# RWKV-7 scan on one core: fewer, fuller TensorE visits per slot, and new positions for transpositions and for the inversion

## The chip, the core and the metric

The kernel runs on one core of one Trainium2 chip. The metric is the device time of one execution in microseconds (us). Before the change the median of three runs is 2085.17 us (2083.7 to 2086.77).

The engines are called as the profile calls them: PE is TensorE (matmuls; PEld its weight loads), DVE is VectorE, ACT is ScalarE, POOL is GpSimd, SP is SyncE, which issues the DMAs.

## The reference, cut to what matters

Two layers on x of shape (1, 512, 2048). Layer 0 is attention and a pooling mixer and isn't touched. Layer 1 is RWKV-7 time mixing with 32 heads of 64 channels; its heart is a recurrence over the 512 tokens:

```python
def step(state, inp):                      # per head: state is 64 x 64
    r_t, w_t, k_t, v_t, kk_t, a_t = inp
    sa = jnp.einsum('bhvk,bhk->bhv', state, -kk_t)
    state = (state * w_t[:, :, None, :]
             + sa[..., None] * (kk_t * a_t)[:, :, None, :]
             + v_t[..., None] * k_t[:, :, None, :])
    return state, jnp.einsum('bhvk,bhk->bhv', state, r_t)
```

After it come a group norm per head, a bonus term, a gate and an output projection.

## The kernel before

**Stages.** Layer 0 and the projections for r, k and g fill the first 1400 us or so. Then comes `scan`, which takes the 32 heads as 16 pairs (two heads of 64 channels fill 128 partitions) and the 512 tokens as 8 chunks of 64. The projection for v is done inside the scan, as filler for PE. The output projection follows.

**What a pair needs.** Per pair q there are these pieces of work, each a Python generator whose steps are called *visits* here:

- `gprod(q)` (line 894): loads AR and BK, and makes the products BK x AR per chunk (line 908, tile `g`, two PSUM banks of four chunks, one bank per head), masked by DVE into `Z` (line 914); then transposes BK on PE (line 920, tile `bt`) and ACT copies it to `BT` (line 921).
- `lanes(q)` (line 945): the first level of inverting the 64 x 64 triangular matrices, in blocks of 16. POOL gathers the blocks from Z into `nd` with four instructions (line 950: two need the Z of one head, two that of the other), DVE transposes `nd` into `lt` (line 955), adds it up to `la`, then fifteen rounds of a product `pr` (line 962) and a sum `uc` (line 963), each of which needs the one before. ACT writes `e` (line 969), DVE transposes it to `tb` (line 971), ACT makes `DT` in two instructions (line 973), DVE transposes DT into `U` (line 977).
- `levels(q)` (line 981): the other two levels, four groups of small matmuls: q1, c1, q2, c2 (lines 1000 and 1010), with ACT and DVE in between. q1 needs DT.
- `vproj(q)` (line 875): the v projection, eight visits of six matmuls (lines 145 to 147, tile `vps`). `vprep(q)` transposes v. `post(q)` does group norm, transposition (`ot`, line 1104) and gate.
- `chain(q)` (line 1029): the recurrence over the eight chunks, which can't be moved. Each chunk takes three positions: **first** `xo` from state M and RS (lines 1044, 1047), copied to `xs` by DVE and then ACT (1051, 1052); **second** `sa` (1055), copied to `RS` by DVE (1056); **third** `s` (1062), from which DVE makes the new M in four instructions (1071), and the outputs `xo` (1076).

**Order of the work.** `slot` (line 1165) goes through 12 positions. At each it emits the next step of the running chains (the second half of pair p and the first half of pair p+1), with high priority, and then all planned visits whose number falls in that position. So positions 0, 3, 6, 9 hold xo and xs, positions 1, 4, 7, 10 hold sa and RS, positions 2, 5, 8, 11 hold s and M. `plan` (line 1161) spreads n visits evenly between two numbers, counted from the slot in which the pair's g begin; numbers from 12 on fall in the slot behind, so that in one slot the g of pair q+1 stand beside the levels of pair q. PE keeps the order in which the code emits; DVE, ACT and POOL are ordered by a list scheduler when the kernel is built, and each engine works through its own list strictly in that order. There are 13 slots in which two chains run and g, lanes, levels and v stand between them (1455 to 1836 us of the trace), one before them with a single chain, and two behind.

Positions of PE's visits in such a slot, by the old numbers: g at 0, 1, 3 and 4 (two chunks of each bank per visit); bt at 6 and 7; q1, c1, q2, c2 at 5, 7, 9, 10; v at 0, 2, 3, 5, 6, 8, 9, 11; ot at 5; the transposition of v at 11.

Of the kernel before, what the change touches and what calls it, by code (L numbers as in the profile page):

```python
# [8 lines left out]
F32 = mybir.dt.float32  # L9
F32R = mybir.dt.float32r  # L10
# [7 lines left out]
P = 128  # L18
S = 512
# [8 lines left out]

PO, LA, VP, LV, GP, VJ = (13.5, 20), (8, 15), (21.5, 25), (16, 24.5), (0.5, 9), (5.5, 17)
Q14, A13, B13, A14, B14, A15, B15, Q15 = (0, 3), (0.5, 5.5), (6, 12), (0, 10), (3, 12), (0, 9), (0.5, 11.5), (0, 11.5)


class Kernel:
# [809 lines left out]
    def scan(self, ctx, xv, first, mp, ld, ar_d, bk_d, bc_d, g_d, m_d):  # L845
# [8 lines left out]
        st = ctx.enter_context(tc.tile_pool(name="set", bufs=3))  # L854
# [39 lines left out]
        def gprod(p):  # L894

            s = sets[p]
            AR = s["AR"] = ld.tile([P, 8, 2, 64], F32, tag="AR", name="AR", bufs=4)
            nc.sync.dma_start(AR.rearrange("p a b c -> p (a b c)"), ar_d[p])
            BK = ld.tile([P, 8, P], F32, tag="BK", name="BK")
            nc.sync.dma_start(BK.rearrange("p a b -> p (a b)"), bk_d[p])  # L900
            yield

            Z = s["Z"] = [st.tile([P, 8, P], F32, tag=f"Z{h}", name=f"Z{h}", bufs=4) for h in range(2)]
            for b in range(2):
                g = [aux("g").rearrange("p (c n) -> p c n", c=4) for _ in range(2)]
                for c in range(4):
                    for h in range(2):
                        mm(g[h][:, c, :], BK[half[h], 4 * b + c, :],  # L908
                           AR[half[h], 4 * b + c].rearrange("p a b -> p (a b)"), start=True, stop=True)
                    if c == 1:  # L910
                        yield
                for h in range(2):
                    mk = self.mk[:, 64 * (p % 2):64 * (p % 2) + P]
                    nc.vector.tensor_mul(Z[h][:, 4 * b:4 * b + 4, :], g[h], mk.unsqueeze(1).to_broadcast([P, 4, P]))
                yield
            BT = s["BT"] = st.tile([P, 8, P], F32, tag="BT", name="BT")
            for b in range(2):
                g = aux("bt")
                for c in range(4):
                    nc.tensor.transpose(g[:, c * P:(c + 1) * P], BK[:, 4 * b + c, :], self.ident)  # L920
                nc.scalar.copy(BT[:, 4 * b:4 * b + 4, :], g.rearrange("p (c n) -> p c n", c=4))
                yield
# [58 lines left out]
        def levels(p):  # L981

            U, DT = (sets[p][n] for n in ("U", "DT"))
            ev = lambda t: t.rearrange("p c (b z t) -> p c b z t", b=2, z=2)[:, :, :, 0, :]
            od = lambda t: t.rearrange("p c (b z t) -> p c b z t", b=2, z=2)[:, :, :, 1, :]
            b2 = lambda g: g.rearrange("p c (b t) -> p c b t", b=2)
            N1 = tp.tile([P, 8, 64], F32, tag="N1", name="N1")

            Z, own, odd = sets[p]["Z"], p % 2, 64 * (p % 2)
            nc.scalar.copy(N1[half[1 - own]], Z[1 - own][half[own], :, odd:odd + 64])  # L990
            N = [N1, N1]
            N[own] = Z[own][:, :, odd:odd + 64]
            yield

            def prod(name, L, R, K=0, n=64, m=0):
                g = pi.tile([P, 8, 32], F32, tag="i", name=name)
                for c in range(8):
                    for h in range(2):
                        kr, mr = slice(64 * h + K, 64 * h + K + n), slice(64 * h + m, 64 * h + m + n)
                        mm(g[mr, c, :], L[h][kr, c, 64 - n:64] if L is N else L[kr, c], R[kr, c], start=True, stop=True)  # L1000
                return g

            g = b2(prod("q1", N, ev(DT)))
            for b in range(2):
                nc.scalar.activation(q1z[:, :, 32 * b:32 * b + 16], g[:, :, b, :], AF.Copy, scale=self.om[:, b:b + 1])
            yield
            g = pi.tile([P, 8, 32], F32, tag="i", name="c1")
            for c in range(8):
                for h in range(2):
                    mm(g[64 * h:64 * h + 48, c, :], q1z[half[h], c, :48], od(U)[half[h], c], start=True, stop=True)  # L1010
            for h in range(2):
                r = slice(64 * h, 64 * h + 48)
                nc.vector.tensor_add(od(U)[r], od(U)[r], b2(g)[r])
            UT = tp.tile([P, 8, 32], F32, tag="UT", name="UT")
            nc.vector.transpose(UT, U[:, :, :32])
            yield
            g = prod("q2", N, UT, 0, 32, 32)
            q2 = tp.tile([P, 8, 32], F32, tag="q2", name="q2")
            for h in range(2):
                r = slice(64 * h + 32, 64 * h + 64)  # L1020
                nc.scalar.copy(q2[r], g[r])
            yield
            g = prod("c2", q2, U[:, :, 32:], 32, 32, 0)
            for h in range(2):
                r = slice(64 * h, 64 * h + 32)
                nc.vector.tensor_add(U[r, :, 32:], U[r, :, 32:], g[r])
            yield

        def chain(p):
# [3 lines left out]
            s = sets[p]  # L1033
            AR, RS, U, BT, Z = (s[n] for n in ("AR", "RS", "U", "BT", "Z"))
            O = s["O"] = tp.tile([P, 4, 2, 64], F32, tag="O", name="O", bufs=3)
# [3 lines left out]
            for c in range(8):  # L1039
# [19 lines left out]
                if c < 7:  # L1059
                    s1 = po.tile([P, 64], F32, tag="o", name="s1")  # L1060
                    for h in range(2):
                        mm(s1[half[h], :], BT[:, c, 64 * h:64 * h + 64], RS[:, c, h, :], start=True, stop=True)  # L1062
                    Mn = Ms[own * 2 + c % 2]
# [57 lines left out]
        wo = {}  # L1121

        def units(*ks):
            for k in ks:
                tag = "AR,Z0,Z1,AR,Z0,Z1,BT,RS,AR,Z0,Z1,BT,RS,BK,AR,Z0".split(",")[k]
                pool = ld if tag in ("AR", "BK") else st
                w = pool.tile([P, 2, S], F32R, tag=tag, name="wo", bufs=1 if k == 13 else 4 if tag[-1] in "R01" and tag != "RS" else 3)
                raw = self.wp.tile([P, S], F32, tag="wraw", name="wraw", bufs=3)
                nc.sync.dma_start(raw, Wo[k * P:(k + 1) * P, 0:512])
                self.split(w[:, 0, :], w[:, 1, :], raw)  # L1130
                if k not in mixed:
                    kk = [q for q in (k, k + 1) if q < 13]
                    ml = ld.tile([P, 2, S], F32, tag="BK", name="ml")
                    for n, q in enumerate(kk):
                        nc.sync.dma_start(ml[:, n, :], m_d[q])
                        mixed[q] = mp.tile([P, 2, S], F32R, tag="mx", name="mixed")
                        self.split(mixed[q][:, 0, :], mixed[q][:, 1, :], ml[:, n, :])
                wo[k] = w
                yield
# [19 lines left out]
        todo = []  # L1159

        def plan(base, g, n, a, b):

            todo.extend((base + a + (b - a) * q / n, len(todo), g) for q in range(n))
# [12 lines left out]
        def hurry(g):  # L1176
            while True:
                with tc.high_priority(offset=400):
                    if next(g, g) is g:
                        return  # L1180
                yield

        def plan_pair(base, q, skip=0):

            gp = gprod(q)
            next(gp)
            plan(base, gp, 6, *GP)
            plan(base, hurry(lanes(q)) if q == 15 else lanes(q), 18, *LA)
            plan(base, hurry(levels(q)) if q == 15 else levels(q), 5, *LV)
            plan(base, vproj(q), 8, *VJ)  # L1190
            plan(base, vprep(q), 2, *VP)


        v, gp = vproj(0), gprod(0)
        next(gp)
        for q in range(3):
# [3 lines left out]
        for q in range(16):  # L1200
            next(la)
            if q % 2:
                next(v, None)
        g1, v = gprod(1), vproj(1)
        next(g1)
        run(la)
        for q in range(6):
            next(g1)
            if q % 2:
                next(v)  # L1210
        run(vprep(0))
# [7 lines left out]
                next(v)  # L1219
        run(l0)  # L1220
        plan(-12, la, 12, 12, LA[1])
        plan(-12, levels(1), 5, *LV)
        plan(-12, vprep(1), 2, *VP)
        A = None
        for p in range(-1, 16):
# [20 lines left out]
        g = post(15)  # L1246
# [89 lines left out]
```

## Time and profile before

| what | value |
|---|---|
| median of three runs | 2085.17 us |
| the profiled execution, its own time | 2082.76 us |
| span in its trace | 2081.1 us |
| PE, PEld, DVE, ACT, POOL busy | 97%, 79%, 62%, 46%, 14% of the span |
| the 13 full slots of the scan | 1455.0 to 1836 us, 29.3 us each |
| granted TensorE clock, mean | 0.992 |

A row of the timeline has the start, the duration, the engine, the line, the operation, output <- inputs and shapes; merged rows carry xcount, and brackets tell how long the engine had idled before it and what released it. A row of the waits tells who waited for whom: the sum in us, how often, the longest. A row of the groups ends with busy time, mean ns of one, and the idle time ahead of it with its releasers. Matmuls are pipelined, so the time from the start of one visit to the start of the next is what a visit costs on PE.

### The profile page before, as it was taken

How to read it: one execution, taken by the hardware profiler on the slowest of the kernel's cores; microseconds unless marked ns; L12 is line 12 of the kernel's file. 1: busy time of each engine (PE TensorE's matmuls, PEld its weight loads, DVE VectorE, ACT ScalarE, POOL GpSimd, SP SyncE). 2: the span in 40 equal slices, each digit the busy share in tenths (PEclk: the TensorE clock that was granted, in tenths of full speed). 3: DMA queues.
4: the chain of work that ended last, by engine and by line, in shares of the span. 5: the costliest groups of instructions: out<-in, count | busy, mean ns of one | idle time of the engine just before them, and what ended most of it. 6: DMA issues, size and time to landing. Idle time of an engine off the chain costs nothing. (4 is left out here: it accounts for less than half of the span.)

```text
span 2081.1 us, 33937 instructions
## 1 busy us (share of the span) xinstructions
PE 2015.5 (97%) x13091; PEld 1635.0 (79%) x13091; DVE 1281.4 (62%) x2572; ACT 960.2 (46%) x1687; POOL 282.9 (14%) x550
## 2 busy tenths in 40 slices
PE   8999999999999998999999999999999999989996
PEld 7888888888888897777878888876777777767786
DVE  4344345444433358666866676668788888876336
ACT  3345445323322138654645564454565555564221
POOL 0000000000000000234000000013444444410003
PEclk9999999999999999999999999999999999999998
DMA  5222222233333353465365556542223332332733
GB/s 195 92 81 81 81 81 66 86 97 99 99 111 112 117 167 125 143 179 175 118 212 194 177 174 218 197 164 67 81 84 108 108 108 84 101 113 97 245 104 111
DMA packets 214033, 262.99 MB, mean 126 GB/s; under 512 B 15768, under 2 KB 161776, under 8 KB 213104
## 3 DMA queue, kind: packets, MB, share of 16 engines
q1 hardware_dynamic: 213872, 260.83, 38.9%
q8 instruction: 103, 1.69, 0.3%
q14 instruction: 58, 0.48, 0.1%
HBM read 214.32 MB, written 46.47 MB: 125 GB/s over the span
## 5 line engine op out<-in xcount | busy, mean ns | idle before, releaser
L141 DVE TENSOR_TENSOR wlo<-wraw,whi 128x1024 fp32r<-128x1024 f32 (+1 forms) x268 | 314.7, 1177 | 464.3 <-ACT whi L137 455.9
L137 ACT CAST whi<-wraw 128x1024 fp32r<-128x1024 f32 (+1 forms) x324 | 302.9, 938 | 538.3 <-PE ga L146 299.6
L145 PE MATMUL ga<-mx,whi 128*128 128x512 f32 x768 | 299.8, 391 | 3.9 <-ACT mx L137 3.9
L146 PE MATMUL ga<-mx,whi 128*128 128x512 f32 x768 | 300.2, 391 | 2.1 <-DVE mx L141 2.1
L145 PE MATMUL ga<-x,whi 128*128 128x512 f32 x768 | 300.5, 391 | 1.0 <-ACT whi L137 1.0
L147 PE MATMUL ga<-mx,wlo 128*128 128x512 f32 x768 | 300.0, 391 | 0.0
L147 PE MATMUL ga<-x,wlo 128*128 128x512 f32 x768 | 299.4, 390 | 0.5 <-DVE wlo L141 0.5
L146 PE MATMUL ga<-x,whi 128*128 128x512 f32 x768 | 299.2, 390 | 0.0
L508 PE MATMUL gb<-wlo,mixed 128*128 128x512 f32 (+1 forms) x576 | 196.9, 343 | 1.8 <-DVE wlo L141 1.8
L506 PE MATMUL gb<-whi,mixed 128*128 128x512 f32 (+1 forms) x576 | 197.4, 343 | 1.1 <-DVE s L457 1.1
L507 PE MATMUL gb<-whi,mixed 128*128 128x512 f32 (+1 forms) x576 | 196.9, 342 | 0.0
L145 PEld LDWEIGHTS ga<-mx,whi 128*128 128x128 f32 x768 | 144.7, 188 | 36.6 <-ACT mx L137 4.1
L146 PEld LDWEIGHTS ga<-mx,whi 128*128 128x128 f32 x768 | 144.7, 188 | 33.7 <-DVE mx L141 2.8
L147 PEld LDWEIGHTS ga<-x,wlo 128*128 128x128 f32 x768 | 144.2, 188 | 31.2 <-DVE wlo L141 1.0
L147 PEld LDWEIGHTS ga<-mx,wlo 128*128 128x128 f32 x768 | 144.6, 188 | 30.5
L145 PEld LDWEIGHTS ga<-x,whi 128*128 128x128 f32 x768 | 144.2, 188 | 30.6 <-ACT whi L137 1.3
L146 PEld LDWEIGHTS ga<-x,whi 128*128 128x128 f32 x768 | 144.3, 188 | 29.1
L141 POOL TENSOR_TENSOR wlo<-wraw,whi 128x128 fp32r<-128x128 f32 x224 | 100.3, 478 | 222.1 <-ACT whi L137 196.7
L508 PEld LDWEIGHTS gb<-wlo,mixed 128*128 128x128 f32 x576 | 109.1, 190 | 15.8 <-DVE wlo L141 3.4
L506 PEld LDWEIGHTS gb<-whi,mixed 128*128 128x128 f32 x576 | 109.1, 190 | 15.3 <-DVE s L457 2.8
L507 PEld LDWEIGHTS gb<-whi,mixed 128*128 128x128 f32 x576 | 109.2, 190 | 12.3
L145 PE MATMUL vps<-mx,whi 128*128 128x512 f32 x256 | 113.4, 443 | 0.8 <-ACT vT L891 0.8
(333 smaller groups left out, 3345.4 us busy)
## 6 DMA issues: line engine op xcount, KB each, us to landing
wraw<-in_ev_w_in SPq DMA_DIRECT2D x96, 512.0 KB, 3.6
wraw<-in_ev_w_out SPq DMA_DIRECT2D x32, 512.0 KB, 3.6
wraw<-in_od_w_k SPq DMA_DIRECT2D x32, 512.0 KB, 4.7
wraw<-in_od_w_r SPq DMA_DIRECT2D x32, 512.0 KB, 3.4
wraw<-in_od_w_g SPq DMA_DIRECT2D x32, 512.0 KB, 3.8
wraw<-in_od_w_v SPq DMA_DIRECT2D x64, 256.0 KB, 2.7
ar_d<-pAR SPq DMA_DIRECT2D x16, 512.0 KB, 2.6
bk_d<-pBK SPq DMA_DIRECT2D x16, 512.0 KB, 3.3
```

Of the source, the lines that this page charges most:

```text
L137: self.nc.scalar.copy(hi, src)
L141: (eng or self.nc.vector).tensor_sub(lo[:, sl], src[:, sl], hi[:, sl].bitcast(F32))
L145: mm(ps, ah, bh, start=start, stop=False)
L146: mm(ps, ah, bl, start=False, stop=False)
L147: mm(ps, al, bh, start=False, stop=stop)
L506: mm(ps, ah, bh, start=start, stop=False)
L507: mm(ps, al, bh, start=False, stop=False)
L508: mm(ps, ah, bl, start=False, stop=stop)
```

## The change

The new kernel has its lines one further down from the table on (line 909 for 908, 1055 for 1056). It does four things.

- g: the yield after the second chunk goes, so one visit makes four chunks of both banks. gprod has four visits and no longer six; they get written-out positions 1.5, 3.3 (g) and 5.45, 6.9 (bt), the latter two just ahead of v's visits at 5.5 and 6.94.
- levels: written-out positions 15.5, 16.5, 19.5, 21.1, 22.5, so q1, c1, q2, c2 stand at 4, 7, 9 and 10 of a slot.
- lanes: 18 visits spread from 6.5 to 14.5, before from 8 to 15.
- BT gets four buffers, before three (4 KB more per partition); the output projection's tiles that share its tag follow.

```diff
-PO, LA, VP, LV, GP, VJ = (13.5, 20), (8, 15), (21.5, 25), (16, 24.5), (0.5, 9), (5.5, 17)
+PO, LA, VP, VJ = (13.5, 20), (6.5, 14.5), (21.5, 25), (5.5, 17)
+LV, GP = (15.5, 16.5, 19.5, 21.1, 22.5), (1.5, 3.3, 5.45, 6.9)
...
                         mm(g[h][:, c, :], BK[half[h], 4 * b + c, :],
                            AR[half[h], 4 * b + c].rearrange("p a b -> p (a b)"), start=True, stop=True)
-                    if c == 1:
-                        yield
...
-            BT = s["BT"] = st.tile([P, 8, P], F32, tag="BT", name="BT")
+            BT = s["BT"] = st.tile([P, 8, P], F32, tag="BT", name="BT", bufs=4)
...
+        def at_(base, g, *where):
+
+            todo.extend((base + x, len(todo), g) for x in where)
...
-            plan(base, gp, 6, *GP)
+            at_(base, gp, *GP)
             plan(base, hurry(lanes(q)) if q == 15 else lanes(q), 18, *LA)
-            plan(base, hurry(levels(q)) if q == 15 else levels(q), 5, *LV)
+            at_(base, hurry(levels(q)) if q == 15 else levels(q), *LV)
```

**PE, position 1 of the slot in which pair 7 ends and pair 8 begins** (`sa` products, then `g`, then `s`). Before:

```order
L1055 MATMUL sa<-xs_10978,U 64x128
L1055 MATMUL sa<-xs_10977,U 64x128
L908 MATMUL g<-AR,BK 128x128 x4
L1062 MATMUL s_14927<-RS,BT 64x64 x2
L1062 MATMUL s_14934<-RS,BT 64x64 x2
```

Now:

```order
L1054 MATMUL sa<-xs_10978,U 64x128
L1054 MATMUL sa<-xs_10977,U 64x128
L909 MATMUL g<-AR,BK 128x128 x8
L1061 MATMUL s_14936<-RS,BT 64x64 x2
L1061 MATMUL s_14943<-RS,BT 64x64 x2
```

The visit between sa and s has all eight products of the two banks; the visit of four at position 0 is gone.

**DVE, positions 2 to 5 of a slot.** Before, from tb to the xs of position 6 (the xs of position 3 stand ahead of these rows):

```order
L971 STREAM_TRANSPOSE tb<-e 128x512
L1056 COPY RS<-sa 64x128 x2
L914 TENSOR_TENSOR Z_14435<-g,mk 128x512
L1071 SCALAR_TENSOR_TENSOR M_10980<-s_14564,pcs,m_14567 64x64 x2
L1071 SCALAR_TENSOR_TENSOR M_10982<-s_14571,pcs,m_14574 64x64 x2
L977 STREAM_TRANSPOSE U<-DT 128x512
L914 TENSOR_TENSOR Z_14436<-g,mk 128x512
L955 STREAM_TRANSPOSE lt<-nd_10975 128x512
L1051 COPY xs_10977<-xo 64x64
L1051 COPY xs_10978<-xo 64x64
```

Now, from tb to the M of position 5 (the xs here are those of position 3):

```order
L970 STREAM_TRANSPOSE tb<-e 128x512
L1050 COPY xs_10977<-xo 64x64
L1050 COPY xs_10978<-xo 64x64
L221 SCALAR_TENSOR_TENSOR rsygn<-rstgn,rssgn 128x8
L1099 TENSOR_TENSOR O<-O,rsygn 128x512
L976 STREAM_TRANSPOSE U<-DT 128x512
L913 TENSOR_TENSOR Z_14459<-g,mk 128x512
L913 TENSOR_TENSOR Z_14460<-g,mk 128x512
L1055 COPY RS<-sa 64x128 x2
L954 STREAM_TRANSPOSE lt<-nd_10975 128x512
L1070 SCALAR_TENSOR_TENSOR M_10980<-s_14583,pcs,m_14586 64x64 x2
L1070 SCALAR_TENSOR_TENSOR M_10982<-s_14590,pcs,m_14593 64x64 x2
```

U and both Z have moved ahead of the chain's RS, the two Z stand next to each other, and lt has moved ahead of the chain's M; before, lt had only the xs of the next position behind it. On ACT the second DT now stands behind the two copies xs of position 3; before, no xs stood between the two DT.

More of the change, by code (lines that the diff above doesn't have):

```diff
@@ L1126, in units @@
                 pool = ld if tag in ("AR", "BK") else st
-                w = pool.tile([P, 2, S], F32R, tag=tag, name="wo", bufs=1 if k == 13 else 4 if tag[-1] in "R01" and tag != "RS" else 3)
+                w = pool.tile([P, 2, S], F32R, tag=tag, name="wo", bufs=1 if k == 13 else 3 if tag == "RS" else 4)
                 raw = self.wp.tile([P, S], F32, tag="wraw", name="wraw", bufs=3)
@@ L1181, in hurry, with plan_pair @@
                 yield
-        def plan_pair(base, q, skip=0):
+        def at_(base, g, *where):
+            todo.extend((base + x, len(todo), g) for x in where)
+        def plan_pair(base, q):
             gp = gprod(q)
             next(gp)
-            plan(base, gp, 6, *GP)
+            at_(base, gp, *GP)
             plan(base, hurry(lanes(q)) if q == 15 else lanes(q), 18, *LA)
-            plan(base, hurry(levels(q)) if q == 15 else levels(q), 5, *LV)
+            at_(base, hurry(levels(q)) if q == 15 else levels(q), *LV)
             plan(base, vproj(q), 8, *VJ)
@@ L1207, in scan @@
         for q in range(6):
-            next(g1)
+            next(g1, None)
             if q % 2:
@@ L1221, in scan @@
         plan(-12, la, 12, 12, LA[1])
-        plan(-12, levels(1), 5, *LV)
+        at_(-12, levels(1), *LV)
         plan(-12, vprep(1), 2, *VP)
```

## The prediction

> **What bounds the kernel now.** I read the page first, then cut out the scan, the only stage that the change touches, and asked who waits for whom there.
>
> ```profile
> PE 2015.5 (97%) x13091; PEld 1635.0 (79%) x13091; DVE 1281.4 (62%) x2572; ACT 960.2 (46%) x1687; POOL 282.9 (14%) x550
> ```
>
> By the whole span this is a kernel of PE: 97% busy, DVE 62%. The stretches of the scan look different. Twelve full slots lie between 1485 and 1836 us (columns: length, then busy time of PE, PEld, DVE, ACT, POOL, the granted clock, DMA); the two slots behind them stand in the second row.
>
> ```profile
> 1485.00:1836.00 351.00, 339.05 (x4323) 254.10 (x4324) 305.86 (x993) 206.93 (x533) 152.48 (x300) 1.00 0.32 100
> 1836.00:1888.80 52.80, 45.95 (x487) 31.50 (x487) 42.04 (x118) 29.48 (x81) 2.05 (x5) 0.90 0.34 109
> ```
>
> A slot is 351.0/12 = 29.25 us, and DVE is busy in 305.86/12 = 25.5 of it, 87%. Who waits, in the same stretch, DVE first and then PE:
>
> ```profile
> DVE lt L955 <- POOL nd L950: 19.6, 12, 1.6
> DVE RS L1056 <- PE sa L1055: 2.6, 4, 0.7
> DVE U L977 <- ACT DT L973: 2.2, 5, 0.5
> DVE tb L971 <- ACT e L969: 1.1, 6, 0.2
> DVE U L1026 <- PE c L1000: 0.4, 1, 0.4
> DVE xs L1051 <- PE xo L1047: 0.2, 1, 0.2
> ```
>
> ```profile
> PE s L1062 <- DVE RS L1056: 7.0, 19, 0.8
> PE q L1000 <- ACT DT L973: 2.3, 4, 0.6
> ```
>
> The sum of DVE's waits is 26.1 us, 2.2 per slot, and 1.63 of that is one wait for POOL, once in each slot. With 25.5 busy and 2.2 waiting, the 1.55 that are left of 29.25 are hand-offs between instructions. For PE, DVE waits 2.6 + 0.4 + 0.2 = 3.2 us in twelve slots; PE waits for DVE twice as long, nearly always at s, for RS. So a slot is as long as DVE's list, with its waits, takes to go round; PE's list is a close second, and its 97% hides that it is held up. What a change to the scan is worth is then read from DVE's list.
>
> **The change part by part: PE.** These rows are from one slot; the start of the next visit less the start of a visit is its cost.
>
> ```profile
> 1600.93 0.71 PE L908 MATMUL g<-AR,BK 64*128 64x128 f32 x8
> 1601.57 0.50 PE L145 MATMUL vps<-mx,whi 128*128 128x512 f32 x1
> ...
> 1616.60 0.66 PE L920 MATMUL bt<-ident,BK 128*128 128x128 f32 x4
> 1617.01 0.48 PE L145 MATMUL vps<-mx,whi 128*128 128x512 f32 x1
> ...
> 1619.93 0.66 PE L920 MATMUL bt<-ident,BK 128*128 128x128 f32 x4
> 1620.52 0.45 PE L1062 MATMUL s<-RS,BT 128*64 128x64 f32 x8
> ```
>
> ```profile
> L908 PE MATMUL g<-AR,BK 64*128 64x128 f32 x384 | 39.1, 300 | 0.0
> ```
>
> A visit of g costs 1601.57 - 1600.93 = 0.64. One matmul record takes 0.30, so the eight of a visit start (0.71 - 0.30)/7 = 0.06 apart, and a visit that takes over the other's eight grows by 0.5. Two visits go and two grow: 2 x (0.64 - 0.5) = 0.3 us per slot saved. The second bt costs 0.59 between c1 and s, and 0.41 ahead of v: 0.2 saved. q1 keeps its work and loses about one switch of shape, 0.1. PE's list thus gets 0.6 us shorter per slot.
>
> The switch itself shows in the weight loads: 0.17 us idle, released by nothing that the profile shows.
>
> ```profile
> 1603.52 0.52 PEld L908 LDWEIGHTS g<-AR,BK 64*128 64x128 f32 x8 [0.17 <-issue]
> ```
>
> [...]
>
> **DVE.** Here the new order adds work to wait for. The rows of the same slot, and the groups:
>
> ```profile
> 1611.28 0.69 DVE L971 STREAM_TRANSPOSE tb<-e 128x512 f32<-128x512 f32 x1
> ...
> 1612.01 0.79 ACT L973 ACTIVATE DT<-tb,qm 128x256 f32<-128x256 f32 x1
> ...
> 1613.77 1.51 POOL L950 TENSOR_TENSOR nd<-Z,md 32x256 f32<-32x256 f32 x2
> ...
> 1614.12 0.71 DVE L977 STREAM_TRANSPOSE U<-DT 128x512 f32<-128x512 f32 x1 [0.47 <-ACT DT L973]
> 1614.85 0.69 DVE L914 TENSOR_TENSOR Z<-g,mk 128x512 f32<-128x512 f32 x1
> ...
> 1615.62 1.51 POOL L950 TENSOR_TENSOR nd<-Z,md 32x256 f32<-32x256 f32 x2 [0.34 <-DVE Z L914]
> ...
> 1617.17 0.71 DVE L955 STREAM_TRANSPOSE lt<-nd 128x512 f32<-128x512 f32 x1 [1.63 <-POOL nd L950]
> 1617.91 0.47 DVE L1051 COPY xs<-xo 64x64 f32<-64x64 f32 x2
> ```
>
> ```profile
> L973 ACT ACTIVATE DT<-tb,qm 128x256 f32<-128x256 f32 x24 | 17.4, 760 | 0.4 <-DVE rstgn L218 0.4
> L1052 ACT COPY xs<-xo 64x64 f32<-64x64 f32 x96 | 19.8, 206 | 37.3 <-DVE xs L1051 35.0
> L1100 DVE TENSOR_TENSOR O<-O,rsygn 128x512 f32<-128x512 f32 x12 | 8.3, 689 | 0.3
> L1056 DVE COPY RS<-sa 64x128 f32<-64x128 f32 x96 | 27.7, 289 | 5.9 <-PE sa L1055 2.6
> ```
>
> *U.* Before, RS, Z and four M lie between tb and U and cover ACT's two DT. Now only two xs (0.47) and O (0.69) do, 1.15 together, while ACT has to do DT, two xs and DT: 0.76 + 2 x 0.21 + 0.76, with three hand-offs 2.05. U waits 0.9, before 0.2 (2.2/12). Queued behind it are both Z and the chain's RS of position 4, for which s on PE waits.
>
> *lt.* Before, POOL has done the first two nd when the second Z ends (1615.54), so lt waits for two, 1.51. Now the two Z stand next to each other: all four nd, 3.03, start when the first of them ends. The second Z, which starts some 0.09 before the first ends and takes 0.69, covers 0.6 and the two RS 2 x 0.29, 1.18 in all; with 0.1 of hand-offs lt waits 1.95, before 1.63: 0.3 more. Queued behind it are now the four M of position 5, which PE's xo of position 6 needs.
>
> The other waits of before, 2.2 - 1.63 - 0.2 = 0.35, may go, since PE's list is shorter. New waits less old: 0.7 + 0.3 - 0.35 = 0.65 us per slot.
>
> *Closer steps.* The rounds of lanes start earlier, and more of them follow each other directly.
>
> ```profile
> 1624.80 0.19 DVE L962 TENSOR_TENSOR pr<-uc,la 128x25 f32<-128x25 f32 x1
> 1625.02 0.18 DVE L963 TENSOR_REDUCE uc<-pr 128x5 f32<-128x25 f32 x1
> ...
> 1629.59 0.25 DVE L962 TENSOR_TENSOR pr<-uc,la 128x100 f32<-128x100 f32 x1
> 1629.75 0.69 DVE L1093 SCALAR_TENSOR_TENSOR O<-gs,O 128x512 f32<-128x512 f32 x1
> ```
>
> The sum that needs pr starts 0.03 after its end; an instruction that needs nothing of it, 0.09 before. Some five pairs more per slot follow directly, at 0.1 each: up to 0.5 slower. Against that stands PE's 0.6: where the hand-offs (1.55) are really short waits for PE, they shrink, by 0.6 at the most. The trace shows neither by itself; being of a size, I let them cancel and keep both ends, 0.05 and 1.15 us per slot.
>
> *The rest.* These rows are a wait of ACT and two groups of DMAs (KB each, median us to landing).
>
> ```profile
> ACT BT L921 <- PE s L1062: 19.4, 12, 1.6
> ```
>
> ```profile
> BK<-bk_d SPq DMA_DIRECT2D x11, 512.0 KB, 4.8
> bv<-bc_d SPq DMA_DIRECT2D x12, 256.0 KB, 2.7
> ```
>
> BT's fourth buffer lets ACT copy at once; before, the copy waited 1.6 per slot for s, but ACT is busy only 207 of 351 us and no row has anyone waiting for BT: I count nothing. On SP the load of BK now goes ahead of bv and waits for the last bt, and bv is queued behind that. BK is wanted at position 1 of the next slot and bv at 9, so that some three positions (7 us) or more cover the 4.8 and 2.7 to landing; were that cover gone, up to 4.8 would show in each slot. Pairs 0 and 1 have their g before the chains run, where DVE isn't full: 2 x 0.3 = 0.6 less in all.
>
> **The sum.** 13 slots x 0.65 = 8.5, less 0.6: 7.9 us slower. On the profiled execution's own 2082.76 that is 2090.7; the median of the runs stands 2.4 above that execution, so 2093.0.
>
> **The rivals.**
>
> *PE's list sets the slot* (faster). Then the 0.6 count in full, and the waits at s (7.0/12 = 0.6), which the longer visits between sa and s cover, go for some two thirds: 1.0 x 13 = 13, which gives 2072. For it: PE at 97%. It decides if DVE has 0.7 of slack in each slot, which its 3.2 us of waiting for PE in 351 deny. [...]
>
> *Both cancel* (no change). DVE's new waits take what the shorter list gives, at the lower end, 0.05 x 13: 2085 to 2087. For it: PE and DVE are within 1 or 2 us of each other per slot.
>
> *Everything adds* (slower still): the closer steps cost their 0.5 and PE's relief brings nothing, 1.15 x 13 = 15: 2100.
>
> *The change doesn't do what it says*: excluded for the visits by the rows of the order (eight products in one); a wait for the second bank in the middle of one would give back part.
>
> The clock is a risk of another kind: 0.90 in the two slots behind, 0.1 x 52.8 = 5 us of PE's pace lost there; I allow 2 to 3 us either way for a dip more or less.
>
> **How the numbers follow.** Slower, by either size: 0.63; no change 0.17; faster 0.20. About 0.2%, 4.2 us, is what a measurement of this kernel can tell from no change. The likeliest case by itself reaches from 2086 to 2102. Going down to 2079 takes in no change and the weaker half of the gain, and leaves out some 1 in 8 below and less above 2102.
>
> **What would show it.** Right: in the waits of DVE, U for DT near 0.9 in every slot and lt for nd near 2.0; PE waiting at s of position 5 for RS and at xo of position 6 for M; a slot near 29.9. Right for PE alone: g in visits of sixteen records that cost about 1.15, bt only ahead of v. Wrong: a slot of 28.5 or less with those waits in it, since then DVE had slack that I took for none; or U and lt without the waits.

## The result, and the profile after

The changed kernel takes 2103.28 us (median of 4 runs, 2101.46 to 2104.92), the kernel before 2085.75 beside it (4 runs): ratio 1.0089, 95% interval 1.0077 to 1.0101. That is 17.5 us slower; 7.9 were forecast, and 2103 lies above the range of 2079 to 2102. The profiled execution took 2103.40, its span is 2101.7 (before 2081.1).

The page's first line looks as it did before:

```profile
PE 2016.7 (96%) x13091; PEld 1637.0 (78%) x13091; DVE 1286.9 (61%) x2572; ACT 960.0 (46%) x1687; POOL 280.0 (13%) x550
```

Counted from the start of xo's visit at position 0, the 13 full slots ran from 1455.00 to 1835.91 before and run from 1455.90 to 1856.57 now: 29.30 and 30.82 each, 19.8 us together. The start is 0.9 later, the two slots behind are 2.5 shorter, and what follows the scan is 2.4 longer: 20.6, the difference of the spans. So nearly all of it is in the slots. The stretches of the twelve slots that were cut before, and of the two behind them (length, busy time of PE, PEld, DVE, ACT, POOL, clock, DMA):

```profile
1486.00:1856.60 370.60, 337.43 (x4322) 252.82 (x4322) 312.66 (x996) 205.86 (x533) 151.17 (x301) 1.00 0.31 96
1856.57:1884.38 27.81, 23.94 (x309) 16.91 (x309) 21.72 (x61) 16.08 (x44) 1.75 (x5) 0.94 0.31 97
1884.38:1906.99 22.61, 20.41 (x180) 13.19 (x179) 18.67 (x51) 13.63 (x38) 0.00 (x0) 1.00 0.34 114
```

The clock is 1.00 in these twelve slots, as before (in the first of the 13 it is 0.94, but that slot took 30.01 us, before 29.97). A slot is 370.6/12 = 30.88; DVE is busy 26.05 of it (before 25.49). Who waits there, DVE and then PE:

```profile
DVE lt L954 <- POOL nd L949: 24.8, 12, 2.2
DVE U L976 <- ACT DT L972: 8.4, 11, 0.9
DVE RS L1055 <- PE sa L1054: 3.3, 14, 0.4
DVE rstgn L220 <- DVE rstgn L219: 0.5, 1, 0.5
```

```profile
PE s L1061 <- DVE RS L1055: 12.8, 25, 0.7
PE sa L1054 <- ACT xs L1051: 8.8, 18, 0.6
PE xo L1043 <- DVE M L1070: 8.7, 29, 0.6
PE xo L1043 <- DVE M L1072: 1.9, 11, 0.2
PE q L999 <- DVE UT L1014: 0.5, 1, 0.5
```

DVE waits 3.08 per slot instead of 2.18: lt 2.07 (1.63), U 0.70 (0.18), RS 0.28 (0.22). PE waits 2.7 per slot, before 11.4/12 = 0.95. Its waits are at s for RS and at xo for M, which stand behind U and lt on DVE, and at sa for xs (8.8, none before), which ACT copies after DVE. The place where both happen, on DVE in one slot, and what PE sees of it:

```profile
1619.07 0.71 DVE L976 STREAM_TRANSPOSE U<-DT 128x512 f32<-128x512 f32 x1 [0.84 <-ACT DT L972]
1619.71 1.25 DVE L913 TENSOR_TENSOR Z<-g,mk 128x512 f32<-128x512 f32 x2
1620.99 0.61 DVE L1055 COPY RS<-sa 64x128 f32<-64x128 f32 x2
1623.56 0.71 DVE L954 STREAM_TRANSPOSE lt<-nd 128x512 f32<-128x512 f32 x1 [1.96 <-POOL nd L949]
1624.20 1.15 DVE L1070 SCALAR_TENSOR_TENSOR M<-s,pcs,m 64x64 f32<-64x64 f32 x4
```

```profile
1611.70 1.16 PE L909 MATMUL g<-AR,BK 64*128 64x128 f32 x16
1612.79 0.45 PE L1061 MATMUL s<-RS,BT 128*64 128x64 f32 x8
...
1621.34 0.65 PE L1061 MATMUL s<-RS,BT 128*64 128x64 f32 x8 [0.62 <-DVE RS L1055]
1621.82 0.40 PE L1075 MATMUL xo<-RS,Z 128*64 128x64 f32 x8
1622.15 0.65 PE L919 MATMUL bt<-ident,BK 128*128 128x128 f32 x4
1622.56 0.48 PE L146 MATMUL vps<-mx,whi 128*128 128x512 f32 x1
```

U's 0.84 and lt's 1.96 are the forecast's 0.9 and 1.95; g in one visit of sixteen costs 1612.79 - 1611.70 = 1.09 (1.15 forecast), and bt ahead of v costs 1622.56 - 1622.15 = 0.41, as forecast. The mechanism is there. What is missing is what was set against it.

### The profile page after: what moved, and what is told of

Its sections match the earlier page's. It is cut to its first block, busy times and chain, and to the rows that moved or that the text cites. A ratio compares the mean times of both kernels' runs of the same rounds, so it can differ in the third digit from the quotient of the medians.

```text
span 2101.7 us, 33927 instructions
## 1 busy us (share of the span) xinstructions
PE 2016.7 (96%) x13091; PEld 1637.0 (78%) x13091; DVE 1286.9 (61%) x2572; ACT 960.0 (46%) x1687; POOL 280.0 (13%) x550
## 3 DMA queue, kind: packets, MB, share of 16 engines
q1 hardware_dynamic: 213872, 260.83, 38.3%
## 5 line engine op out<-in xcount | busy, mean ns | idle before, releaser
L147 PEld LDWEIGHTS ga<-x,whi 128*128 128x128 f32 x768 | 144.4, 188 | 29.3
L507 PEld LDWEIGHTS gb<-whi,mixed 128*128 128x128 f32 x576 | 109.5, 190 | 15.5 <-DVE s L458 2.9
```

The lines of the kernel that those rows point to most:

```text
L147: mm(ps, ah, bl, start=False, stop=False)
L507: mm(ps, ah, bh, start=start, stop=False)
```

## The experiments

A slot can be written as DVE's busy time, its waits and the rest, which holds the hand-offs between its instructions. These three add up to the slot by construction; what can be tested is whether the slot shrinks when one of them does. The table holds that account for twelve slots of each run (e7 stands apart), worked out from the row of the stretch and the sum of DVE's waits; the last column is the sum of PE's waits, all per slot.

| run | us | slot | DVE busy | DVE waits | rest | PE waits |
|---|---|---|---|---|---|---|
| before | 2085.75 | 29.25 | 25.49 | 2.18 | 1.58 | 0.95 |
| after | 2103.28 | 30.88 | 26.05 | 3.08 | 1.75 | 2.73 |
| e1 g alone | 2107.31 | 31.25 | 26.63 | 2.64 | 1.99 | 2.27 |
| e2 lanes and levels alone | 2117.95 | 32.33 | 25.75 | 4.96 | 1.62 | 2.32 |
| e3 lt behind M | 2106.17 | 31.33 | 26.31 | 3.28 | 1.75 | 3.04 |
| e4 U behind RS | 2071.02 | 28.31 | 26.23 | 0.32 | 1.77 | 0.86 |
| e5 lt behind M, nd whole | 2087.28 | 29.61 | 26.52 | 1.32 | 1.77 | 2.01 |
| e6 no wlo | 2096.90 | 30.57 | 25.69 | 3.15 | 1.74 | 2.35 |
| e8 before, less DVE | 2066.62 | 28.44 | 22.45 | 4.43 | 1.57 | 0.39 |
| e9 after, less DVE | 2079.70 | 29.53 | 22.64 | 5.28 | 1.61 | 1.77 |
| e10 U behind RS, POOL in halves | 2069.96 | 28.27 | 25.98 | 0.58 | 1.71 | 0.70 |
| e11 after, more PE | 2100.21 | 30.71 | 26.12 | 2.82 | 1.77 | 1.82 |
| e12 U behind RS, more PE | 2074.88 | 28.61 | 26.31 | 0.63 | 1.67 | 0.75 |

The first theory, D: DVE's list, with what stands in it ahead of RS and M, is the slot. Its rival, L: the new positions of lanes and levels do the harm, whatever DVE's order.

**e1, the merged visits of g alone** (on the kernel before):

```diff
-PO, LA, VP, LV, GP, VJ = (13.5, 20), (8, 15), (21.5, 25), (16, 24.5), (0.5, 9), (5.5, 17)
+PO, LA, VP, LV, GP, VJ = (13.5, 20), (8, 15), (21.5, 25), (16, 24.5), (1.5, 3.3, 6.17, 7.58), (5.5, 17)
...
-                    if c == 1:
-                        yield
...
-            plan(base, gp, 6, *GP)
+            todo.extend((base + x, len(todo), gp) for x in GP)
...
```

> The kernel before with only the merged visits of g (eight products in one, at 1.5 and 3.3; bt at its old 6.17 and 7.58, three buffers of BT, lanes and levels where they were). DVE's list in it: in one slot of two U and both Z stand ahead of RS and lt ahead of M, as in the changed kernel; in the others lt stands behind M and one Z ahead of U. Theory D (DVE's list is the bound, and the merged visits push U, Z and lt ahead of the chain's RS and M): half of the 1.5 us per slot that the change costs, or a little more, so 13 x 0.9 = 12 us: 2097 us (2091 to 2102). Theory L (the new positions of lanes and levels do the harm: q1 right behind sa, lanes begun before M of position 5): no harm here, PE's 0.3 us per slot shorter: 2081 to 2086 us.

Measured 2107.31 (2105.0 to 2108.85), ratio 1.0107 [1.0092, 1.0122]. Its slots alternate; two of them at full clock:

```profile
1611.89:1642.16 30.27, 28.19 (x361) 21.00 (x361) 26.22 (x84) 17.01 (x45) 12.23 (x26) 1.00 0.31 97
1642.16:1674.40 32.24, 28.86 (x362) 21.20 (x361) 27.19 (x85) 16.90 (x45) 12.98 (x26) 1.00 0.29 92
```

In the first lt stands behind the four M and waits 0.87; in the second both Z stand ahead of RS and lt ahead of M, and lt waits 2.17. U waits 0.9 in both. So the order that the changed kernel has in every slot is the slower of the two here by 1.97. **e2, the new positions of lanes and levels alone** (on the kernel before):

```diff
-PO, LA, VP, LV, GP, VJ = (13.5, 20), (8, 15), (21.5, 25), (16, 24.5), (0.5, 9), (5.5, 17)
+PO, LA, VP, LV, GP, VJ = (13.5, 20), (6.5, 14.5), (21.5, 25), (15.5, 16.5, 19.5, 21.1, 22.5), (0.5, 9), (5.5, 17)
...
+            lv = hurry(levels(q)) if q == 15 else levels(q)
...
-            plan(base, hurry(levels(q)) if q == 15 else levels(q), 5, *LV)
+            todo.extend((base + x, len(todo), lv) for x in LV)
...
```

> The kernel before with only the new positions of lanes (6.5 to 14.5) and levels (15.5, 16.5, 19.5, 21.1, 22.5); g and bt as before. DVE's list keeps RS ahead of both Z, M ahead of lt, and U right behind RS with some cover. Theory D: within some 4 us of the kernel before, 2082 to 2090 us. Theory L: most of the harm is here, 2096 to 2104 us.

Measured 2117.95 (2114.72 to 2124.04), ratio 1.0163 [1.0141, 1.0184]. e2 by itself is slower than the whole change, and e1 no faster (the intervals of their ratios overlap); both theories miss both numbers. In e2 PE waits at q1 for DT; the two steps there, and the stretches around them with the clock in the third column from the right:

```profile
1591.99 0.44 PE L1055 MATMUL sa<-xs,U 128*64 128x128 f32 x4
1594.45 0.24 PE L1000 MATMUL q<-DT,Z 64*64 64x32 f32 x1 [2.02 <-ACT DT L973]
```

```profile
1592.00:1594.00 2.00, 0.43 (x5) 0.18 (x4) 1.19 (x3) 1.98 (x4) 1.40 (x4) 1.00 0.00 0
1594.00:1596.00 2.00, 1.55 (x32) 1.55 (x32) 0.71 (x1) 0.40 (x1) 0.29 (x1) 0.65 0.30 86
1596.00:1598.00 2.00, 2.00 (x26) 1.71 (x26) 0.53 (x1) 0.62 (x2) 0.00 (x0) 0.50 0.19 53
1598.00:1600.00 2.00, 2.00 (x14) 1.60 (x11) 1.90 (x6) 1.21 (x4) 1.45 (x2) 0.50 0.00 0
1600.00:1602.00 2.00, 2.00 (x12) 1.44 (x12) 0.37 (x1) 0.08 (x1) 1.47 (x2) 0.65 0.00 0
```

Here, after 2.0 us without a matmul, the granted clock is 0.50 for some 7 us. PE waits as long at q1 in nearly every slot of e2 (24.0 us in twelve), but not each wait is followed by as much: the slots have clocks of 0.90 and 0.95 by turns, which is about 6.7 and 3.1 us at half clock, and the last has 1.00. In e1, where PE waits up to 1.7 us at s, three slots fall to 0.90 and 0.95. So e1 and e2 each have a price that the whole change has not (clock 1.00), and don't split its 17 us. Over the twelve slots the clock took at most (1 - 0.93) x 388 = 27 us of e2's 34, but only (1 - 0.98) x 375 = 8 of e1's 23 (estimates from the mean clock): the merged visits of g alone, without the clock, cost about as much as the whole change.

**e3, lt queued behind the four M of position 5** (on the changed kernel; m_ins is the newest M):

```diff
-            nc.vector.transpose(lt.rearrange("p a b -> p (a b)"), nd2.rearrange("p a b -> p (a b)"))
+            with tc.issue_after(self.m_ins.ins) if p > 2 else ExitStack():
+                nc.vector.transpose(lt.rearrange("p a b -> p (a b)"), nd2.rearrange("p a b -> p (a b)"))
...
```

> The changed kernel with one thing more: DVE's list is held so that lt stands behind the newest M (order of issue alone, no wait for M to end), so position 5 has RS, M, M, lt and no longer RS, lt, M, M. U still waits for DT. Theory D: the four M (1.2 us) cover part of the 1.96 us for which lt waits, which leaves 0.8 or so, and PE's xo at position 6 no longer waits for M; a slot falls from 30.8 to 29.7: 13 x 1.1 = 14 us less than the changed kernel, 2089 us (2085 to 2095). Theory L: PE's order is the same, so 2100 to 2104 us.

Measured 2106.17 (2103.4 to 2108.61), ratio 1.0102 [1.0085, 1.012]: above both ranges, and D's gain didn't come. Its clock is 0.98 over the twelve slots, so up to 0.02 x 376 = 8 us of this time may be the clock's. **e4, U visited later and queued behind RS** (on the changed kernel; both Z now stand right behind O, so POOL's nd start earlier, and the scheduler puts M ahead of lt by itself):

```diff
-            nc.vector.transpose(U.rearrange("p a b -> p (a b)"), DT.rearrange("p a b -> p (a b)"))
+            with tc.issue_after(self.rs_ins.ins) if p > 1 else ExitStack():
+                nc.vector.transpose(U.rearrange("p a b -> p (a b)"), DT.rearrange("p a b -> p (a b)"))
...
-            plan(base, hurry(lanes(q)) if q == 15 else lanes(q), 18, *LA)
+            ln = hurry(lanes(q)) if q == 15 else lanes(q)
+            at_(base, ln, *[LA[0] + (LA[1] - LA[0]) * x / 18 for x in range(17)], 16.2)
```

> The changed kernel with U (the transposition of DT) visited at position 4 of the next slot and held behind RS of that position on DVE; both Z then stand right behind O, and the list scheduler itself puts M ahead of lt. PE's order is that of the changed kernel. Theory D: neither wait is left (U under 0.1, lt under 0.5 us per slot), DVE's list is its 25.5 to 26 us busy and some 1.8 of hand-offs and small waits, a slot 28.4 us; 13 x 2.4 = 31 us less than the changed kernel, 2072 us (2066 to 2082), faster than the kernel before too. Theory L: 2100 to 2104 us.

Measured 2071.02 (2068.5 to 2071.59), ratio 0.9932 [0.9917, 0.9946]: faster than both kernels. The waits of DVE in e4 and in e3, and POOL in one slot of e3:

```profile
DVE lt L954 <- POOL nd L949: 3.5, 7, 2.2
DVE RS L1056 <- PE sa L1055: 0.3, 2, 0.2
```

```profile
DVE lt L955 <- POOL nd L949: 27.2, 12, 2.7
DVE U L977 <- ACT DT L973: 5.2, 11, 0.7
```

```profile
1590.25 2.31 POOL L949 TENSOR_TENSOR nd<-Z,md 32x256 f32<-32x256 f32 x3 [7.01 <-DVE Z L913]
1592.64 1.70 POOL L142 TENSOR_TENSOR wlo<-wraw,whi 128x128 fp32r<-128x128 f32 x4
1594.42 0.74 POOL L949 TENSOR_TENSOR nd<-Z,md 32x256 f32<-32x256 f32 x1
```

In e4 the waits are gone (0.32 per slot, 2.76 less), and the slot is 2.57 shorter. It moves U, Z, M and lt at once and doesn't say what each is worth. In e3 the scheduler, with lt later, had let four wlo pass the last nd: 1.70 us, so that lt waited 2.27 although M's four stood ahead of it. The edit had taken a wait off the list and put it back on POOL. **e5 mends that**: nd is visited at position 5.4, ahead of wlo, lt where it was and behind M; DVE's order is e3's.

```diff
+            if p > 2:
+                yield
             lt = tp.tile([P, 16, 32], F32, tag="i3", name="lt")
...
+            ln = hurry(lanes(q)) if q == 15 else lanes(q)
+            if q > 2:
+                at_(base, ln, 5.4)
```

> The changed kernel with lt queued behind the four M of position 5, as in the run with lt behind M, but with POOL's four nd kept together: in that run the last nd had slipped behind the four wlo, 1.7 us, and lt waited 2.27 us per slot for it (27.2/12). Theory S (a slot is the sum of DVE's busy time, hand-offs and waits): with nd whole, the four M cover 1.2 of lt's 2.07 (24.8/12), lt waits 0.9, the slot falls from 30.88 by 1.2 to 29.7, 13 x 1.2 = 15.6, so 2088 (2082 to 2094). Rival (U's wait with RS behind it is all that harms, and lt's place is worth nothing): 2100 to 2106, like the changed kernel.

Measured 2087.28 (2085.41 to 2090.0), ratio 1.0011 [1.0002, 1.0021].

```profile
DVE lt L957 <- POOL nd L949: 9.9, 12, 1.6
DVE U L979 <- ACT DT L975: 5.2, 11, 0.7
```

lt waits 0.83, expected 0.9; the time is within a microsecond of the sum. That it is so close is in part luck: U and RS wait 0.5 less too, and DVE's busy time grew by 0.46. e3 and e5 differ by where POOL's fourth nd stands, and by 18.9 us, e3's clock included. Theory S, that a wait taken out of DVE's list shortens the slot by about its length, replaces D.

**e6, no wlo on POOL.** The busy time of DVE had grown by 0.56 per slot, which the waits don't tell. The group of one instruction, in the kernel before, in the changed kernel, and in e6:

```profile
L218 DVE TENSOR_TENSOR rstgn<-rssgn 128x8 f32<-128x8 f32 x12 | 2.0, 168 | 0.0
```

```profile
L219 DVE TENSOR_TENSOR rstgn<-rssgn 128x8 f32<-128x8 f32 x12 | 4.2, 348 | 0.2
```

```profile
L219 DVE TENSOR_TENSOR rstgn<-rssgn 128x8 f32<-128x8 f32 x12 | 1.9, 162 | 0.2
```

The next count takes each row of DVE's timeline that is over 0.12 us longer than the shortest of its form in any run, and adds up what it is longer by. In twelve slots there are 15 before, 3.8 us, and 47 after, 10.1 us, nearly all pr and rstgn, whose two operands lie in SBUF, and all of them beside an instruction of POOL, mostly wlo (33 of the 47). That is 0.5 per slot of the 0.56. The rounds, which start earlier, now run when POOL splits weights. The edit:

```diff
-        for q in range(parts):
+        for q in range(0 if eng else parts):
...
-                self.mm3(ps, wh[:, k % 4, :], wl[:, k % 4, :], xv[k][:, 0, :], xv[k][:, 1, :], k == 0, k == NK - 1)
+                self.mm3(ps, wh[:, k % 4, :], (wh if p > 1 else wl)[:, k % 4, :], xv[k][:, 0, :], xv[k][:, 1, :], k == 0, k == NK - 1)
```

> The changed kernel without wlo on POOL in v's projection (from pair 2 on the product with wlo takes whi in its place, so that PE does the same work on other numbers). Theory P (DVE's small products of two SBUF operands, pr and rstgn, are stretched while POOL runs its own): in the changed kernel 33 of them beside wlo are 0.12 to 0.27 longer than the shortest of their shape, 6.4 us in 12 slots, in the kernel before 14 with 3.6. Without wlo the 0.53 per slot go from DVE's busy time (26.05 to 25.5), 13 x 0.53 = 7, so 2096 (2093 to 2099). Rival (the busy time grew because dependent steps follow each other closer): DVE's busy time stays at 26.0 and the time at 2101 to 2106.

Measured 2096.9 (2094.51 to 2100.42), ratio 1.0057 [1.004, 1.0074]; DVE's waits didn't change (3.15), its busy time fell to 25.69, 0.36 less: by the same count 16 long rows with 4.2 us are left, all beside bv. DVE's product rstgn took a mean of 348 ns in the changed kernel and 162 without wlo; whether it stands still or goes slower beside POOL, no row shows.

**e7, less work for PE, and e8, less for DVE** (both on the kernel before): the third product of v's projection left out; rounds 9 to 15 left out.

```diff
-                self.mm3(ps, wh[:, k % 4, :], wl[:, k % 4, :], xv[k][:, 0, :], xv[k][:, 1, :], k == 0, k == NK - 1)
+                mm(ps, wh[:, k % 4, :], xv[k][:, 0, :], start=k == 0, stop=False)
+                mm(ps, wl[:, k % 4, :], xv[k][:, 0, :], start=False, stop=k == NK - 1)
```

```diff
             for t in range(1, 16):
+                if t > 8:
+                    yield
+                    continue
```

> The kernel before with the third product of v's projection left out (what goes into v is less exact): PE has 16 products of 128x512 less per slot, 3.7 us; some 10 us more may go ahead of the scan, so it is judged by the slot (29.25 before). Theory S (DVE's list is the slot, PE's list is not): only DVE's waits for PE, 3.2 us in 12 slots, can go: 28.9 to 29.2 per slot, and a relief of 0.6 on PE is worth 0.1 at most. Rival (PE's list sets the slot): 25.6 to 26.5 per slot.

> The kernel before with rounds 9 to 15 of lanes left out (the inverse of a block is then not finished): DVE has some 14 instructions and 4.3 us less per slot; judged by the slot (29.25 before). Theory S (DVE's list is the slot): the slot falls until PE's list holds it, which the fastest run so far bounds at 27.5 + 0.6 = 28.1 from above: 27.0 to 28.2 per slot. Rival (PE's list sets the slot): 29.2 to 29.4 per slot.

e7 took 2106.76 (2 runs, ratio 1.0103 [1.0078, 1.0128]): PE has 3.7 us less to do in each slot (16 products, whose starts lie 0.23 apart in the kernel before), and the kernel is slower. Three of its slots:

```profile
1513.28:1540.67 27.39, 25.44 (x346) 18.48 (x345) 22.90 (x71) 16.71 (x45) 12.91 (x26) 1.00 0.31 99
1540.67:1577.53 36.86, 28.52 (x346) 21.41 (x345) 29.06 (x98) 17.02 (x45) 12.53 (x26) 0.81 0.27 86
1577.53:1604.81 27.28, 25.46 (x345) 18.49 (x344) 22.82 (x71) 16.72 (x45) 12.92 (x26) 1.00 0.33 100
```

```profile
PE q L1001 <- ACT DT L974: 6.7, 1, 6.7
```

PE runs ahead, stands 6.7 us at q1, and its clock is 0.81 in that slot. The mean slot, 375.07/12 = 31.26, is neither theory's; what PE's list is worth in the kernel before isn't settled by e7. e8 took 2066.62 (2 runs, ratio 0.991 [0.989, 0.9931]); its slots are 28.1 (28.0 to 28.4 from the third to the twelfth; the last, at a clock of 0.95, is 31.3 and makes the table's mean 28.44), in the range of S. DVE's busy time fell by 3.0 per slot and the slot by 1.2 only: below that something else holds it, with PE waiting only 0.4 per slot. PE's list of before is thus some 28, and the slot of before 1.2 longer.

**e9, the same cut as e8 in the changed kernel**, asks if PE's list got shorter.

> The changed kernel with rounds 9 to 15 of lanes left out (the inverse of a block is then not finished), the same cut as in the kernel before with less for DVE, whose slots became 28.1 us, PE's list. Judged by the slot, since the work ahead of the scan shrinks too. Theory S (the change did make PE's list 0.6 us shorter per slot, but DVE's list, not PE's, is the slot of the changed kernel): with DVE's list out of the way the slot comes to 28.1 - 0.6 = 27.5 (27.3 to 27.8). Rival (PE's list did not get shorter): 28.0 to 28.2.

Measured 2079.7 (2077.89 to 2083.51), ratio 0.9974 [0.9963, 0.9985]: slots of 29.3 (the last, at a clock of 0.95, is 32.8), which neither had. PE waits there, 21.2 us in 354.3:

```profile
PE xo L1046 <- DVE M L1073: 7.0, 11, 0.7
PE sa L1057 <- ACT xs L1054: 6.2, 18, 0.4
PE q L1002 <- DVE UT L1017: 3.2, 7, 1.7
PE s L1064 <- DVE RS L1058: 2.9, 7, 0.4
```

Without its waits PE's list is (354.3 - 21.2)/12 = 27.8, in e4 (339.8 - 10.3)/12 = 27.5, in e8 (341.3 - 4.7)/12 = 28.05: by these estimates there is a relief of 0.3 to 0.6. But the slot with less work for DVE still is 1.2 longer in the changed kernel than in that of before, though DVE is busy only 22.6 of it, 3.4 less, and waits 3.0 for PE at RS. The row for M points to lt, which still waits 1.4 per slot with M behind it: it looks as if a wait in DVE's list held up PE's chain here although DVE wasn't full. That is more than S says, and it was not tested by moving lt here; S is right only where DVE's list is dense.

**e10, POOL's wlo and bv in halves, in e4's kernel** (64 columns for 128):

```diff
...
-            for q in range(4):
-                nc.gpsimd.tensor_mul(bv[:, q * P:q * P + P], s["vT"][:, q * P:q * P + P], bv[:, q * P:q * P + P])
+            for q in range(0, S, 64):
+                nc.gpsimd.tensor_mul(bv[:, q:q + 64], s["vT"][:, q:q + 64], bv[:, q:q + 64])
...
```

> The changed kernel with U behind RS (2071.0, slot 28.3) and with POOL's wlo and bv in instructions of half the size, 64 columns for 128, twice as many. Theory P (a product of two SBUF operands on DVE that comes while POOL is inside an instruction waits for its end): the stretches, 53 of them with 13.7 us in 12 slots of that run, get about half as long, 0.4 to 0.6 off a slot, so 2065 (2062 to 2068). Rival (the stretch is a slower rate while both run, whatever the length of POOL's instructions, or POOL's fixed cost per instruction makes up for it): 2069 to 2074.

Measured 2069.96 (2068.08 to 2072.71), ratio 0.9928 [0.9904, 0.9953], like e4. By the count of e6 the stretches went from 53 with 13.8 us to 56 with 9.8: shorter, as P says, though not half (64 columns of wlo took POOL a mean of 335 ns, 128 took 467 in the changed kernel). But DVE's busy time, 0.25 per slot less, buys nothing here: DVE waits 0.26 more, for sa. The time lies in the rival's range, and a slower rate as the cause of the stretch isn't excluded.

**e11 and e12, more work for PE**, in the changed kernel and in e4's: three more products in each slot.

```diff
+                for _ in range(3 if k in (13,) and p > 1 else 0):
+                    mm(ps, wh[:, k % 4, :], xv[k][:, 0, :], start=False, stop=False)
```

> The changed kernel with PE's list made longer again by as much as the change shortened it: three more products of 128x512 per slot at one place of v's projection (what goes into v is changed), 3 x 0.23 = 0.7 us. In the changed kernel PE waits 32.7 us in twelve slots, 2.7 per slot, for DVE and ACT. Theory S (DVE's list with its waits is the slot, PE's relief brought nothing): the 0.7 go into PE's waits, 2103 (2100 to 2106). Rival (PE's list is worth its time here, and without the relief the change would have been slower still): 13 x 0.7 = 9, so 2112 (2109 to 2115).

> The same three products, 0.7 us of PE per slot, in the changed kernel with U behind RS (2071.0). There PE waits only 10.3 us in twelve slots, 0.86 per slot, and halving POOL's instructions took 0.3 per slot off DVE's list without a gain. Theory PE (with DVE's waits gone, PE's list is the slot, and this is where the change's 0.6 would count): 13 x 0.7 = 9, so 2080 (2077 to 2082). Rival (DVE's list is the slot here too): 2070 to 2073.

e11 took 2100.21 (2096.01 to 2101.62), ratio 1.0067 [1.0046, 1.0089]: 0.7 us more PE per slot cost nothing. PE's waits fell from 32.7 to 21.8 us in twelve slots:

```profile
PE sa L1056 <- ACT xs L1053: 9.1, 19, 0.5
PE xo L1045 <- DVE M L1072: 6.8, 22, 0.6
PE s L1063 <- DVE RS L1057: 5.4, 15, 0.6
```

It is even 3 us quicker, with U waiting 5.1 instead of 8.4: the scheduler had put O ahead of xs. So DVE's order changed too, and U's 0.28 per slot, 13 x 0.28 = 3.6 us, is about what the run gained. e12 took 2074.88 (2071.77 to 2075.65), ratio 0.9948 [0.9932, 0.9965]: 3.9 of the 9 us. If relief is worth what added work costs, the 0.6 are worth nothing in the changed kernel, and something like 0.4 of themselves once U's and lt's waits are gone; neither theory of e12 holds alone, as if DVE's and PE's lists in e4 were of nearly one length.

## Why the prediction was wrong

*What bounds the scan*: right for the changed kernel, with a limit. Taking waits out of DVE's list gave 2.6 us per slot (e4), and giving PE more cost nothing (e11), though PE's busy share is 96%. But DVE isn't simply full: with 3.4 us less to do (e9) the slot fell by 1.35 only.

*U and lt*: right, and the larger part of it. U 0.52 more per slot (0.7 forecast; in the row of one slot 0.84 for 0.9), lt 0.44 (0.3). e4 and e5 show that these waits cost about their length.

*The other waits of before, 0.35, may go*: they did not; RS alone waits 0.28. The sum of DVE's waits grew by 0.90 instead of 0.65.

*Closer steps against PE's relief, "being of a size, I let them cancel"*: this is the step that failed. PE's relief came out about as counted (g 1.09, bt 0.41) and was worth nothing (e11), which the text's own argument on DVE's list should have told. The 0.1 of q1, for a switch of shape, no row shows by itself: PE waits right behind q1 (0.62 at s, above). On the other side stood 0.56 of busy time and 0.17 of hand-offs. Closer steps are at most half of it: without wlo (e6) busy time and rest stand 0.20 and 0.16 above before, and rows of pr and uc that follow each other directly went from 172 to 199 in the twelve slots, 2.3 more per slot where the prediction takes five. The other 0.36 (0.5 by the count of long rows) was the stretching of pr and rstgn beside POOL, a term that the prediction didn't have. The kernel before shows it in one product of nearly every slot, beside wlo, against the same product in the changed kernel:

```profile
1627.20 0.45 DVE L962 TENSOR_TENSOR pr<-uc,la 128x81 f32<-128x81 f32 x1
```

```profile
1633.09 0.25 DVE L961 TENSOR_TENSOR pr<-uc,la 128x81 f32<-128x81 f32 x1
```

Together 0.90 + 0.56 + 0.17 = 1.63 per slot by the stretches, 1.52 by xo's starts, x 13 = 19.8. *Everything adds* (1.15 per slot, 2100) was the nearest of the rivals, right on PE's relief, but in part by luck: its 0.5 for closer steps stands where stretching did the larger part. *PE's list sets the slot* (2072) is excluded by the result and by e11. That e4's 2071 comes near 2072 is another thing: there the waits are gone by DVE's order.

*BT's buffer and SP's queue*: no cost seen; ACT's wait for s at BT (19.4 us before) is gone, and nobody gained. *The clock*: 2.5 us came back in the two slots behind, at 0.94 and 1.00 for 0.88 and 0.93, the size that was allowed for.

Open stays why half the clock comes after idle stretches of 2.0 us in e2, for some 3 or some 7 us or not at all, and what PE's list is worth in the kernel before, where e7 lost its clock.

## What to carry to other kernels

A wait in DVE's list cost what stood behind it (e4: 2.76 us of waits less, a slot 2.57 shorter): before visits are merged on one engine, write down the order that this gives on the engine that is the bound, and look what its first waiting instruction holds back. A saving on an engine that waits was worth nothing here as long as it waited (e11: 0.7 us more for PE in each slot, 2100.21 for 2103.28), and must not be set against a cost on the engine that is waited for. The remedy was small: the waiting step visited later, and one dependence that puts it behind the chain's step.

## What the hardware showed unexpectedly

Less work made the kernel slower: with 3.7 us less for PE per slot (e7, 2106.76 for 2085.14) PE stood idle up to 6.7 us at a time (38.3 us in six waits) and its clock was 0.81 to 0.90 in every other slot. In e2 2.0 us of idleness were followed by some 7 us at half clock in every other slot and by half of that in the slots between; in the last of the twelve the clock stayed at 1.00.

Two small products of DVE, pr and rstgn, took longer beside POOL's instructions, up to twice their time and more: rstgn took a mean of 162 ns without wlo, 348 in the changed kernel, 409 in e4.
